# One kernel, two transformer layers of each of two kinds: experts' products kept together on TensorE, weights asked for earlier, low queries padded to full depth

## The chip, the cores and the metric

The kernel runs on one core of a Trainium2 chip. A core has five engines, each with its own queue of instructions: TensorE (PE, with its weight loader PEld), VectorE (DVE), ScalarE (ACT), GpSimd (POOL) and SyncE (SP, which issues most of the DMA transfers). The metric is the time on the device in microseconds (us), the median of the runs.

## The reference

The input is 512 tokens of 1024 numbers. Two layers of a first kind come first, then two of a second kind, all in float32.

A layer of the first kind projects the normed tokens, runs three mixers beside each other (an mLSTM in chunks, a causal attention with compressed keys, a gating over chunks), projects their outputs back and adds them to the tokens. After that comes a mixture of 32 experts, of which each token goes to two:

```python
def expert_block(args):
    rows, rw, e = args
    xi = x_pad[rows]
    h = jax.nn.silu(xi @ w1[e]) * (xi @ w3[e])
    return (h @ w2[e]) * rw[:, None]
```

Here w1 and w3 are 1024 x 256 and w2 is 256 x 1024 for each expert.

A layer of the second kind has an attention (dilated with 16 heads in the first, differential with 8 double heads in the second), a cross attention to 256 memory tokens and a feed-forward block. The scores of both attentions are a product of queries and keys over 64 numbers per head:

```python
sc = jnp.einsum('bhcqd,bhckd->bhcqk', qblk, k, preferred_element_type=f32) * scale
p = jax.nn.softmax(sc, axis=-1)
```

## The kernel before, in words

**Order of the work.** The class `Kern` writes every instruction to a `Recorder` (lines 86 to 381) in place of issuing it. `add` (157) notes what each operation reads and writes and derives from it what it depends on; `price` (209) gives its cost by engine and shape. At the end `flush` (245) plays the program through these costs and decides the order of each engine. For every engine it takes the ready operations, keeps those that can start by the earliest time at which any of them can, and picks the one of lowest rank (316). The rank is the place in the program, in steps of AGE (100, and 1000 within `moe`), less the operation's height, which is the cost of the longest chain behind it (286 to 291). Buffers are part of that plan: an operation that needs a new tile waits for a free slot of the pool (268 to 284). The order found is then issued, with the order on each engine fixed (366 to 378). The prices hold no cost for a change of a product's shape. All instructions of the program therefore bear the line of this issuing loop, L367, in the profile, and they are told apart by their tiles.

**Buffers.** The heap is 46 tiles of 128 x 1024 float32 (`H`, 470); `T2` gives half tiles, and all eight banks of PSUM are one pool (515, 518). Most products are made of three, with high and low halves of both operands in a rounded format (`mm3`, 534); weights come as `raw` and are split into `wh` and `wl` (`wload`, 561).

**Experts.** `run` (2260) does for each of the first two layers: the mixers and output projection (`f1`), the routing (`route`), the keys and values of a memory (`mem_kv`, whose results are stored to DRAM as `memk` and `memv`), the twelve loads of the first pair's weights (`pair_raw`, 2126, called at 2272), the overflow loop (`overflow`, 2044) and the experts (`moe`, 2145). The overflow loop is a wall: it is recorded as an operation of all engines (2102), reads its count on all of them, and starts when all are free; operations behind it in the program can be planned ahead of it only if its buffers stay free (280). Experts are worked on in 16 pairs per layer, 64 slots for each expert of the pair. For a pair, `prep_pair` (2175) gathers the 128 rows of tokens with an indirect DMA on POOL into `xg` and transposes them in eight blocks into `xe`; `up` (2187) does 32 products with w1 and w3, `down` (2202) transposes the result and does eight products with w2, and after every second pair `combine` (2226) adds the results to the tokens by eight sums of four products each. The two experts of a pair lie on the two halves of the output's partitions, so each product of `up` and `down` has 64 columns of weights:

```python
mm(ps[e * 64:(e + 1) * 64, g * 256:(g + 1) * 256], x[:, j * 128 + e * 64:j * 128 + (e + 1) * 64],
   w[:, j % 4 * 256:(j % 4 + 1) * 256], start=j == 0, stop=j == 7)
```

In the profile these are `mm<-raw,xe` (up, two instructions for each product) and `mm<-raw,t` (down, two as well); the combine products are `mm<-yh,pT` and `mm<-yl,pT`. The planner is free to set any other ready product between two of these.

**Attention.** `qkv_steps` (1084) projects queries, keys and values for half of the heads at a time (hb). For a block of 128 tokens it turns the queries by the rotary angles on POOL (1103), transposes them on TensorE and writes a high part `qh` on ScalarE (1115) and a low part `ql` on VectorE (1118). Of the even heads the high part of the query lies on partitions 0 to 63 and again on 64 to 127, against keys whose high part lies on one half of the partitions and whose low part on the other. The low query lies on its own 64 partitions alone, two blocks of tokens in one tile. `qk` (1133) is the product of both for a head: one product over 128 rows with `qh` (`mm<-kt,qh`) and one over 64 rows with `ql` (`mm<-kt,ql`):

```python
s.nc.tensor.matmul(out, q[:, e * 512 + h // 2 * 128:e * 512 + (h // 2 + 1) * 128], k[:, o], start=True, stop=False)
s.nc.tensor.matmul(out, l[a, h // 2 * 128:(h // 2 + 1) * 128], k[a, o], start=False, stop=True)
```

`longnet` (1141) and `diff` (1229) call it 64 times each, 128 in all, between the projections of the second half of the heads and the output projection of the first.

Of the kernel before, what the change touches and what calls it, by code (L numbers as in the profile page):

```python
# [10 lines left out]
F32 = mybir.dt.float32  # L11
# [54 lines left out]


class Op:
    __slots__ = ("i", "eng", "fn", "a", "k", "cost", "lat", "deps", "users", "left", "ready", "end", "new", "uses", "start", "rows", "load", "move", "age", "height", "rank")


class Engine:
# [13 lines left out]
class Recorder:  # L86
# [15 lines left out]
    def __init__(s, nc, tc):  # L102
        s.nc, s.tc = nc, tc
        s.ops, s.hist, s.first, s.keys = [], {}, {}, {}
        s.tensor, s.vector, s.scalar = Engine(s, "PE", nc.tensor), Engine(s, "DVE", nc.vector), Engine(s, "ACT", nc.scalar)
        s.gpsimd, s.sync = Engine(s, "POOL", nc.gpsimd), Engine(s, "SP", nc.sync)
        s.cache = {}


    def region(s, ap):  # L110
# [46 lines left out]
    def add(s, eng, method, fn, a, k, outs=None, ins=None):  # L157
        o = Op()
        if outs is None:
            outs = [v for n in ("out", "accum_out") for v in s.aps(k.get(n))]  # L160
            rest = list(a)
            if "out" not in k:
                outs += s.aps(rest.pop(0))
            ins = [v for x in rest for v in s.aps(x)] + [v for n, x in k.items() if n not in ("out", "accum_out") for v in s.aps(x)]
        o.i, o.eng, o.fn, o.a, o.k = len(s.ops), eng, fn, a, k
        o.age = s.AGE
        o.cost, o.lat = s.price(eng, method, outs, ins, k)
        o.move = None
        if isinstance(o.cost, tuple):

            o.move, (o.cost, o.lat) = (o.cost[1], o.lat), (o.cost[0], o.cost[1] + o.lat + 900)
        o.deps, o.users, o.new, o.uses = set(), [], [], []
        if eng == "PE":
            m = 1
            for v in ins[0].shape[1:]:
                m *= int(v)
            o.rows, o.load = int(ins[0].shape[0]) / 128, m * 0.417 * (1 if ins[0].dtype == BF16 else 4 if ins[0].dtype == F32 and method == "matmul" else 2)
        for ap, wr in [(x, False) for x in ins] + [(x, True) for x in outs]:
            t = ap.tensor
            if t.space == bass.MemoryType.DRAM and not hasattr(t, "cap_key"):  # L180
                continue
            name = t.name
            p0, p1, m = s.region(ap)
            h = s.hist.setdefault(name, ([], []))
            if t.space != bass.MemoryType.DRAM:
                if name not in s.first:
                    s.first[name] = o
                    tag = ((t.space, t.cap_key), name.split("_")[0] if t.space == PSUM else "")
                    s.keys.setdefault(tag, (int(t.bufs or t.tag_meta.bufs), []))[1].append(name)
                    o.new.append((name, tag))  # L190
                if name not in o.uses:
                    o.uses.append(name)
            for q, q0, q1, qm in h[0]:
                if q1 > p0 and p1 > q0 and qm & m:
                    o.deps.add(q)
            if wr or t.space == PSUM:

                for q, q0, q1, qm in h[1]:
                    if q1 > p0 and p1 > q0 and qm & m and (wr or s.ops[q].eng != eng):
                        o.deps.add(q)  # L200
            if wr:
                for x in h:
                    x[:] = [r for r in x if r[1] < p0 or r[2] > p1 or r[3] & ~m]
            h[wr is False].append((o.i, p0, p1, m))
        o.deps.discard(o.i)
        s.ops.append(o)
# [38 lines left out]
    def flush(s):  # L245
        ops = s.ops
        left = {}
        for o in ops:
            for n in o.uses:
                left[n] = left.get(n, 0) + 1  # L250
            o.left, o.ready, o.end = len(o.deps), 0.0, None
            for d in o.deps:
                ops[d].users.append(o)
# [40 lines left out]
        def next_wall():  # L294
# [6 lines left out]
                    n[tag_of[x][0]] = n.get(tag_of[x][0], 0) + 1  # L301
            return o.i, n
        wall, asked = next_wall()
        while len(order) < len(ops):
            best = None
            for e, hp in heaps.items():
                cand = []
                for i, o in hp[:s.WINDOW]:
                    t = start(o)
                    if t is not None:  # L310
                        cand.append((t, o))
                if not cand:
                    continue
                now = max(free.values()) if e == "ALL" else free[e]
                lim = max(now, min(c[0] for c in cand))
                t, o = min((c for c in cand if c[0] <= lim), key=lambda c: c[1].rank)
                pick = (t, o.i, o)
                if best is None or pick[:2] < best[:2]:
                    best = pick
            t, i, o = best  # L320
            heaps[o.eng].remove((i, o))
            o.new = [(n, tag_of[n]) for n in o.uses if n not in live]
            for n, tag in o.new:
                live.add(n)
# [132 lines left out]
class Kern:  # L457
# [626 lines left out]
    def qkv_steps(s, act, W, hb, kinds, Q, K, values, ready):  # L1084
# [4 lines left out]
        for kind in kinds:  # L1089
            toks = []  # L1090

            def consume(t, ps):
# [10 lines left out]
                s.apply_rope(nc.gpsimd, tok.rearrange("p (h c) -> p h c", h=8)[:, :, 0:16], s.rope2, t, 8, 8)  # L1103
                if kind == 0:
                    q = s.H(F32R, "qh")
                    l = s.H(F32R, "ql") if t % 2 == 0 else Q[hb, t - 1][2]
                    lv = l[:, (t % 2) * 512:(t % 2 + 1) * 512]
                    Q[hb, t] = q, lv, l
                    tp = s.TP()
                    for c in range(4):  # L1110
                        nc.tensor.transpose(tp[:, c * 128:(c + 1) * 128], tok[:, c * 128:(c + 1) * 128], s.ident)
                    for d in range(2):
                        for e in range(2):
                            a, b = slice(64 * e, 64 * e + 64), slice(64 * (e ^ d), 64 * (e ^ d) + 64)
                            nc.scalar.copy(q[b, e * 512:(e + 1) * 512], tp[a])
                    for e in range(2):
                        a, o = slice(64 * e, 64 * e + 64), slice(e * 512, e * 512 + 512)
                        nc.vector.tensor_sub(lv[a], tp[a], q[a, o])
                    return
                for c in range(4) if t == NT - 1 else ():  # L1120
                    tp = s.TP()
# [10 lines left out]

    def qk(s, out, Q, K, hb, t, h):

        q, l, _ = Q[hb, t]
        k, e = K[hb * 4 + h // 2], h % 2
        a, o = slice(64 * e, 64 * e + 64), slice(e * 512, e * 512 + 512)
        s.nc.tensor.matmul(out, q[:, e * 512 + h // 2 * 128:e * 512 + (h // 2 + 1) * 128], k[:, o], start=True, stop=False)
        s.nc.tensor.matmul(out, l[a, h // 2 * 128:(h // 2 + 1) * 128], k[a, o], start=False, stop=True)

    def longnet(s, act, nxt, xsrc):
        nc = s.nc
# [1002 lines left out]
    def moe(s, l, raws, nxt):  # L2145
# [40 lines left out]

        def up(p, w13):
            ps, x = s.PS("pa"), xe.pop(p)
            for g in range(2):
                for j in range(8):  # L2190
                    for e in range(2):
                        w = w13[g * 4 + j // 4 * 2 + e]
                        mm(ps[e * 64:(e + 1) * 64, g * 256:(g + 1) * 256], x[:, j * 128 + e * 64:j * 128 + (e + 1) * 64],
                           w[:, j % 4 * 256:(j % 4 + 1) * 256], start=j == 0, stop=j == 7)
            u = us[p] = s.T2()
            A.activation(u[:, 0:256], ps[:, 0:256], AF.Tanh, scale=0.5)
            V.scalar_tensor_tensor(u[:, 0:256], u[:, 0:256], 1.0, ps[:, 0:256], op0=ALU.add, op1=ALU.mult)
# [4 lines left out]
        def down(p):  # L2202
# [4 lines left out]
            A.copy(u[:, 256:512], tp[:, 0:256])  # L2207
            yb = s.PS("py"), s.PS("py")
            w = w2.pop(p)
            for hf in range(2):  # L2210
                for j in range(2):
                    for e in range(2):
                        mm(yb[hf][e * 64:(e + 1) * 64], u[:, 256 + j * 128 + e * 64:256 + j * 128 + (e + 1) * 64],
                           w[j * 2 + e][:, hf * 512:(hf + 1) * 512], start=j == 0, stop=j == 1)
            g, i = divmod(p, 4)
            _, tok, gate, _ = info[g]
            yh, yl = s.H(F32R, "yh"), s.H(F32R, "yl")
# [8 lines left out]
        def combine(last):  # L2226
            for t in range(NT):
                for hf in range(2):
                    pc = s.PS("pc")
                    n = len(ycur)  # L2230
                    for i, (pT, yh, yl) in enumerate(ycur):
                        for q, yy in enumerate((yh, yl)):
                            mm(pc, pT[:, t * 128:(t + 1) * 128], yy[:, hf * 512:(hf + 1) * 512], start=i == 0 and q == 0,
                               stop=i == n - 1 and q == 1)
                    xs = s.x[t][:, hf * 512:(hf + 1) * 512]
                    V.tensor_add(xs, xs, pc)
                if last:
                    nxt(t)
# [21 lines left out]
    def run(s):  # L2260
# [7 lines left out]
        for l in range(2):  # L2268
            s.f1(l, c.act, s.chain_route(l), I["x"][0] if l == 0 else s.xd)
            s.route()  # L2270
            kv.append(s.mem_kv(l))
            raws = [s.pair_raw(l, 0)]
            s.overflow(l)
            c = s.chain(I["attn_norm"][1] if l == 0 else I["mix_pre_g_2"][0], s.spill)
            s.moe(l, raws, c)
# [25 lines left out]
```

## Time and profile before

| | us |
|---|---|
| median of 3 runs | 2879.23 (2877.32 to 2879.76) |
| the profiled execution | 2878.05 |
| its span, first to last instruction | 2875.6 |
| first expert stage, about | 335 to 640 |
| second expert stage, about | 970 to 1275 |
| attention of the third layer, low queries in use | 1358 to 1560 |
| attention of the fourth layer, low queries in use | 2160 to 2335 |

The profile gives for each engine its busy time, for each group of instructions by tiles and shape (`out<-in partitions*columns`) their number and mean duration, the chain of work that ended last (followed back from the last instruction, at each step to what released it), and the instructions in order of time. A TensorE product's record runs from its start to a modelled end and overlaps the next one's, so durations are longer than the step from one start to the next; steps between starts are what TensorE's time is made of. The weight loader (PEld) works beside the products.

### The profile page before, as it was taken

The numbers are of one execution on the slowest core, as the hardware profiler recorded it, in microseconds if no ns is written. First come the engines' busy times: TensorE is split into PE (matmuls) and PEld (weight loads), VectorE is DVE, ScalarE is ACT, GpSimd is POOL, SyncE is SP. The second block draws the span as 40 slices with busy tenths as digits, with TensorE's granted clock in tenths as the row PEclk, the third lists the DMA queues.
The fourth block names the chain that finished last, engine by engine and source line by source line (L and its number), as shares of the span: only waits on it lengthen the run. The fifth ranks groups of instructions, "written<-read, shape, count | busy, mean of one in ns | idle before, by whom it ended". The sixth has DMA issues, their size and how long they took to land.

```text
span 2875.6 us, 40755 instructions
## 1 busy us (share of the span) xinstructions
PE 2796.2 (97%) x15208; PEld 2166.7 (75%) x15208; DVE 1519.1 (53%) x3279; ACT 1178.3 (41%) x2414; POOL 619.4 (22%) x720
## 2 busy tenths in 40 slices
PE   8999999999999999999999999999999999999998
PEld 7878655559888655557777888888877778888887
DVE  6686433337686243344588564343447685633433
ACT  5565111115555011135587462242356664622421
POOL 2523000003423000002344221001224442210012
PEclk9999999999999999999999999999999999999999
DMA  6035899953135799951013232232321232312321
GB/s 171 23 94 171 302 352 351 374 180 117 39 117 192 275 402 338 363 194 51 30 52 126 85 105 67 81 117 78 122 82 44 67 110 81 108 62 88 118 83 57
DMA packets 224057, 421.94 MB, mean 147 GB/s; under 512 B 46064, under 2 KB 112368, under 8 KB 223856
## 3 DMA queue, kind: packets, MB, share of 16 engines
q1 hardware_dynamic: 219248, 410.89, 41.3%
q0 software_dynamic: 4608, 8.40, 0.8%
q8 instruction: 122, 2.00, 0.3%
q14 instruction: 79, 0.65, 0.1%
HBM read 410.83 MB, written 16.78 MB: 149 GB/s over the span
## 4 chain that ended last, share of the span: by engine, by line
PE 80%; DVE 4%; ACT 2%; POOL 1%; DMA 1%; issue 1%; DVEq 0%; another core or an unknown queue 0%; POOLq 0%; ACTq 0%
PE mm L367 74%; PE tp L367 7%; DVE wl L367 1%; ACT t L367 1%; DVE x L367 1%; DMA raw<-w 1%; DVE t L367 1%; DMA xg<-xm,slidx 0%; POOL ra L367 0%; DVE y L367 0%; ACT qh L367 0%; ACT wh L367 0%; POOL pring L367 0%; DVE xnm L367 0%; DVE n_r L367 0%
## 5 line engine op out<-in xcount | busy, mean ns | idle before, releaser
L367 PE MATMUL mm<-wh,xth 128*128 128x512 f32 (+3 forms) x1088 | 406.6, 398 | 0.0
L367 PE MATMUL mm<-wl,xth 128*128 128x512 f32 (+3 forms) x1088 | 403.7, 396 | 0.8 <-DVE wl L367 0.8
L367 PE MATMUL mm<-wh,xtl 128*128 128x512 f32 (+3 forms) x1088 | 403.5, 395 | 0.0
L367 PE MATMUL mm<-xth,wh 128*128 128x512 f32 (+2 forms) x1216 | 377.7, 361 | 0.2
L367 PE MATMUL mm<-xtl,wh 128*128 128x512 f32 (+2 forms) x1216 | 376.4, 359 | 0.0
L367 PE MATMUL mm<-xth,wl 128*128 128x512 f32 (+2 forms) x1216 | 375.6, 359 | 0.0
L367 DVE SCALAR_TENSOR_TENSOR wl<-raw,pre_g,wh 128x512 fp32r<-128x512 f32 (+4 forms) x400 | 287.8, 760 | 149.5 <-ACT wh L367 119.5
L367 PE MATMUL mm<-raw,xe 128*64 128x256 f32 x2048 | 294.2, 387 | 0.0
L367 ACT ACTIVATE wh<-raw,pre_g 128x512 fp32r<-128x512 f32 (+4 forms) x400 | 251.8, 684 | 62.4 <-DMA raw<-w_gate_up 47.0
L367 PEld LDWEIGHTS mm<-xth,wh 128*128 128x128 f32 (+1 forms) x1216 | 222.6, 188 | 35.5 <-ACT xth L367 0.7
L367 PEld LDWEIGHTS mm<-xtl,wh 128*128 128x128 f32 (+1 forms) x1216 | 222.8, 187 | 35.0 <-issue 0.3
L367 PEld LDWEIGHTS mm<-xth,wl 128*128 128x128 f32 (+1 forms) x1216 | 222.6, 187 | 35.2 <-issue 0.3
L367 PEld LDWEIGHTS mm<-wh,xth 128*128 128x128 f32 x1088 | 204.4, 188 | 38.0 <-issue 5.9
L367 PEld LDWEIGHTS mm<-raw,xe 128*64 128x64 f32 x2048 | 157.1, 137 | 100.6 <-issue 30.0
L367 PEld LDWEIGHTS mm<-wl,xth 128*128 128x128 f32 x1088 | 204.2, 189 | 37.0 <-issue 4.6
L367 PEld LDWEIGHTS mm<-wh,xtl 128*128 128x128 f32 x1088 | 204.4, 188 | 35.9 <-issue 3.9
L367 POOL TENSOR_TENSOR ffl<-t,ffh 128x512 fp32r<-128x512 f32 x44 | 60.6, 1380 | 543.9 <-ACT ffh L367 505.9
L367 DVE TENSOR_TENSOR wl<-raw,wh 128x1024 fp32r<-128x1024 f32 x112 | 143.5, 1286 | 51.7 <-ACT wh L367 47.4
L367 PE MATMUL mm<-raw,t 128*64 128x512 f32 x512 | 137.3, 614 | 7.5 <-ACT t L367 7.4
L367 DVE TENSOR_TENSOR x<-x,mm 128x512 f32<-128x512 f32 x136 | 91.3, 684 | 84.6 <-PE mm L367 84.3
L367 ACT CAST wh<-raw 128x1024 fp32r<-128x1024 f32 (+2 forms) x128 | 120.1, 953 | 33.3 <-DMA raw<-w_down 31.2
L367 DVE SCALAR_TENSOR_TENSOR yl<-mm,slgate,yh 128x512 fp32r<-128x512 f32 x64 | 47.8, 749 | 161.1 <-ACT yh L367 151.1
(337 smaller groups left out, 4961.9 us busy)
## 6 DMA issues: line engine op xcount, KB each, us to landing
raw<-w SPq DMA_DIRECT2D x384, 512.0 KB
raw<-w_gate_up SPq DMA_DIRECT2D x176, 256.0 KB
raw<-w_down SPq DMA_DIRECT2D x40, 512.0 KB
raw<-x_wkv SPq DMA_DIRECT2D x32, 512.0 KB
raw<-a_w_in SPq DMA_DIRECT2D x24, 512.0 KB
raw<-b_w_in SPq DMA_DIRECT2D x24, 512.0 KB
raw<-w_in SPq DMA_DIRECT2D x24, 384.0 KB
raw<-w_out SPq DMA_DIRECT2D x16, 512.0 KB
```

The costliest lines, as they stand in the source:

```text
L367: r = o.fn(*o.a, **o.k)
```

## The change

Four things are changed. The recorder gets `together`: operations recorded within it form a group; the first of the group takes over the dependences on operations ahead of the group and all tiles of the others, and once it is placed, its engine takes the rest of the group next, in order. `up` makes two groups (w1, w3) of 16 products, `down` one of eight, `combine` one of four for each of its sums. `run` calls `pair_raw` for two pairs ahead of the overflow loop. The low queries get a tile of their own for each block, laid out like one copy of the high ones; the 64 partitions that hold nothing are filled with zeros on POOL, and `qk` takes both products over 128 rows.

```diff
+    def together(s, fn, *a):
+        s.run = object()
+        fn(*a)
+        s.run = None
...
     def flush(s):
+        head = None
+        for o in ops:
+            if o.group is None or head is None or head.group is not o.group:
+                head = last = o
+                continue
+            head.deps |= {d for d in o.deps if d < head.i}
+            head.uses += [n for n in o.uses if n not in head.uses]
+            o.deps.add(last.i)
+            last.next = last = o
...
-                for i, o in hp[:s.WINDOW]:
+                for i, o in hp[:s.WINDOW] if forced.get(e) is None else [(forced[e].i, forced[e])]:
...
+            forced[o.eng] = o.next
...
                 if kind == 0:
                     q = s.H(F32R, "qh")
-                    l = s.H(F32R, "ql") if t % 2 == 0 else Q[hb, t - 1][2]
-                    lv = l[:, (t % 2) * 512:(t % 2 + 1) * 512]
-                    Q[hb, t] = q, lv, l
+                    l = s.H(F32R, "ql")
+                    Q[hb, t] = q, l
+                    for e in range(2):
+                        nc.gpsimd.memset(l[64 - 64 * e:128 - 64 * e, e * 512:(e + 1) * 512].bitcast(F32), 0.0)
...
-                        nc.vector.tensor_sub(lv[a], tp[a], q[a, o])
+                        nc.vector.tensor_sub(l[a, o], tp[a], q[a, o])
...
-        s.nc.tensor.matmul(out, q[:, e * 512 + h // 2 * 128:e * 512 + (h // 2 + 1) * 128], k[:, o], start=True, stop=False)
-        s.nc.tensor.matmul(out, l[a, h // 2 * 128:(h // 2 + 1) * 128], k[a, o], start=False, stop=True)
+        for i, x in enumerate(Q[hb, t]):
+            s.nc.tensor.matmul(out, x[:, e * 512 + h // 2 * 128:e * 512 + (h // 2 + 1) * 128], k[:, e * 512:(e + 1) * 512], start=i == 0, stop=i == 1)
...
-            for g in range(2):
+            def part(g):
                 for j in range(8):
                     for e in range(2):
                         w = w13[g * 4 + j // 4 * 2 + e]
...
+            for g in range(2):
+                nc.together(part, g)
...
-            raws = [s.pair_raw(l, 0)]
+            raws = [s.pair_raw(l, p) for p in range(2)]
```

The loops of `down` and of `combine` (over the products of one sum) are wrapped in the same way.

## Rows read from the trace of the kernel before

**Rows 1.** The page, the chain that ended last, by engine.

```profile
PE 80%; DVE 4%; ACT 2%; POOL 1%; DMA 1%; issue 1%; DVEq 0%; another core or an unknown queue 0%; POOLq 0%; ACTq 0%
```

**Rows 2.** Groups by shape, TensorE: tiles, shape, count | busy us, mean ns | idle.

```profile
L367 PE MATMUL mm<-raw,xe 128*64 128x256 f32 x2048 | 294.2, 387 | 0.0
...
L367 PE MATMUL mm<-kt,ql 64*128 64x512 f32 x128 | 61.4, 499 | 0.0
```

**Rows 3.** Windows: length, busy PE, PEld, DVE, ACT, POOL, granted clock, DMA share, GB/s.

```profile
335.00:640.00 305.00, 292.51 (x1797) 168.94 (x1796) 98.38 (x197) 43.04 (x82) 13.78 (x14) 0.99 0.86 323
970.00:1275.00 305.00, 292.69 (x1782) 167.35 (x1781) 95.84 (x183) 42.35 (x80) 12.89 (x13) 0.99 0.86 327
1358.00:1560.00 202.00, 201.70 (x1020) 149.22 (x1018) 139.86 (x319) 143.35 (x300) 88.33 (x102) 1.00 0.16 53
2160.00:2335.00 175.00, 172.58 (x847) 125.69 (x846) 133.21 (x328) 112.91 (x239) 78.71 (x82) 0.98 0.17 55
```

**Rows 4.** Timeline, TensorE, first expert stage: start us, us from first start to last end.

```profile
379.24 0.65 PE L367 MATMUL mm<-raw,xe 128*64 128x256 f32 x2
379.82 0.38 PE L367 MATMUL tp<-const,xg 128*128 128x128 f32 x1
380.12 0.65 PE L367 MATMUL mm<-raw,xe 128*64 128x256 f32 x2
380.70 0.49 PE L367 MATMUL tp<-const,xg 128*128 128x128 f32 x2
```

**Rows 5.** Timeline, TensorE, later in the same stage.

```profile
456.23 0.39 PE L367 MATMUL mm<-yh,pT 128*128 128x512 f32 x1
456.55 1.95 PE L367 MATMUL mm<-raw,xe 128*64 128x256 f32 x16
458.43 0.73 PE L367 MATMUL mm<-yl,pT 128*128 128x512 f32 x2
459.00 0.39 PE L367 MATMUL mm<-yh,pT 128*128 128x512 f32 x1
459.23 0.40 PE L367 MATMUL mm<-yl,pT 128*128 128x512 f32 x1
```

**Rows 6.** Timeline, TensorE: first and last visit of 64 columns (of 173).

```profile
335.20 1.11 PE L367 MATMUL mm<-raw,xe 128*64 128x256 f32 x2
...
1271.64 3.70 PE L367 MATMUL mm<-raw,t 128*64 128x512 f32 x16 [0.46 <-ACT t L367]
```

**Rows 7.** Timeline, TensorE, attention of the fourth layer.

```profile
2272.10 0.40 PE L367 MATMUL mm<-wl,xth 128*128 128x512 f32 x1
2272.34 0.40 PE L367 MATMUL mm<-kt,qh 128*128 128x512 f32 x1
2272.66 0.50 PE L367 MATMUL mm<-kt,ql 64*128 64x512 f32 x1
2273.09 0.50 PE L367 MATMUL mm<-wh,xtl 128*128 128x512 f32 x1
2273.43 0.40 PE L367 MATMUL mm<-wh,xth 128*128 128x512 f32 x1
```

**Rows 8.** Timeline, weight loader, the same stretch; in brackets the idle time before.

```profile
2272.11 0.19 PEld L367 LDWEIGHTS mm<-kt,qh 128*128 128x128 f32 x1
2272.66 0.18 PEld L367 LDWEIGHTS mm<-kt,ql 64*128 64x128 f32 x1 [0.36 <-issue]
```

**Rows 9.** SP's first issues of experts' weights; two pieces of the chain (start, us).

```profile
290.74 0.87 SPq L367 DMA_DIRECT2D raw<-w  x2
...
324.11 7.10 DMA xg<-xm,slidx
...
465.89 6.41 DMA raw<-w
```

**Rows 10.** Windows, end of the fourth layer's attention, columns as in rows 3.

```profile
2300.00:2350.00 50.00, 49.50 (x277) 37.94 (x277) 47.29 (x116) 33.03 (x70) 26.45 (x19) 1.00 0.27 91
```

**Rows 11.** Groups by shape, GpSimd: tiles, shape, count | busy us, mean ns | idle.

```profile
L367 POOL TENSOR_TENSOR pring<-pring,l 128x512 f32<-128x512 f32 x80 | 87.0, 1091 | 184.2 <-DVE l L367 131.5 <-issue 23.9 <-PE mm L367 13.3
```

More of the change, by code (lines that the diff above doesn't have):

```diff
@@ L68 @@
 class Op:
-    __slots__ = ("i", "eng", "fn", "a", "k", "cost", "lat", "deps", "users", "left", "ready", "end", "new", "uses", "start", "rows", "load", "move", "age", "height", "rank")
+    __slots__ = ("i", "eng", "fn", "a", "k", "cost", "lat", "deps", "users", "left", "ready", "end", "new", "uses", "start", "rows", "load", "move", "age", "height", "rank", "group", "next")
 class Engine:
@@ L106, in __init__ @@
         s.gpsimd, s.sync = Engine(s, "POOL", nc.gpsimd), Engine(s, "SP", nc.sync)
-        s.cache = {}
+        s.cache, s.run = {}, None
+    def together(s, fn, *a):
+        s.run = object()
+        fn(*a)
+        s.run = None
     def region(s, ap):
@@ L165, in add @@
         o.i, o.eng, o.fn, o.a, o.k = len(s.ops), eng, fn, a, k
-        o.age = s.AGE
+        o.age, o.group, o.next = s.AGE, s.run, None
         o.cost, o.lat = s.price(eng, method, outs, ins, k)
@@ L303, in flush @@
         wall, asked = next_wall()
+        forced = {}
         while len(order) < len(ops):
@@ L1133, in qk @@
     def qk(s, out, Q, K, hb, t, h):
-        q, l, _ = Q[hb, t]
         k, e = K[hb * 4 + h // 2], h % 2
-        a, o = slice(64 * e, 64 * e + 64), slice(e * 512, e * 512 + 512)
-        s.nc.tensor.matmul(out, q[:, e * 512 + h // 2 * 128:e * 512 + (h // 2 + 1) * 128], k[:, o], start=True, stop=False)
-        s.nc.tensor.matmul(out, l[a, h // 2 * 128:(h // 2 + 1) * 128], k[a, o], start=False, stop=True)
+        for i, x in enumerate(Q[hb, t]):
+            s.nc.tensor.matmul(out, x[:, e * 512 + h // 2 * 128:e * 512 + (h // 2 + 1) * 128], k[:, e * 512:(e + 1) * 512], start=i == 0, stop=i == 1)
     def longnet(s, act, nxt, xsrc):
@@ L2209, in down, with part @@
             w = w2.pop(p)
[L2210 to L2214, printed above, removed]
+            def part():
+                for hf in range(2):
+                    for j in range(2):
+                        for e in range(2):
+                            mm(yb[hf][e * 64:(e + 1) * 64], u[:, 256 + j * 128 + e * 64:256 + j * 128 + (e + 1) * 64],
+                               w[j * 2 + e][:, hf * 512:(hf + 1) * 512], start=j == 0, stop=j == 1)
+            nc.together(part)
             g, i = divmod(p, 4)
@@ L2229, in combine, with part @@
                     pc = s.PS("pc")
[L2230 to L2234, printed above, removed]
+                    def part():
+                        n = len(ycur)
+                        for i, (pT, yh, yl) in enumerate(ycur):
+                            for q, yy in enumerate((yh, yl)):
+                                mm(pc, pT[:, t * 128:(t + 1) * 128], yy[:, hf * 512:(hf + 1) * 512], start=i == 0 and q == 0,
+                                   stop=i == n - 1 and q == 1)
+                    nc.together(part)
                     xs = s.x[t][:, hf * 512:(hf + 1) * 512]
```

## The prediction, as it was made before the result

> **What bounds the kernel now.** I read the page first. TensorE holds 80% of the chain that ended last, and no other engine more than 4% [rows 1]. So the order of TensorE's work is the time, and the question is what in that order is not arithmetic. The groups by shape name the three products that the change touches: the experts' up products (64 columns wide), the experts' down products (64 wide too) and the product with the low queries (64 rows deep) [rows 2, 6]. All others fill 96 or 128 rows and more than 64 columns of weights. I call a stretch of TensorE's order that holds only 64-column products, or only 64-row ones, a visit. The windows then show where they lie: two expert stages of 305 us each and two attention stages of 202 and 175 us, with TensorE busy in 96 to 100% of each [rows 3].
>
> The timeline gives the price of a visit. In the first expert stage one up product (two instructions) alternates with one transpose, and the period from one visit to the next is 380.12 - 379.24 = 0.88 us [rows 4]. In long visits an instruction costs 0.108 us, because two experts' products run side by side: from 456.55 to 458.43 sixteen of them take 1.88 us [rows 5], which is 16 x 0.108 = 1.73 and 0.15 for getting in. A turn with one transpose shows 0.38 and one with two 0.49, so a transpose costs 0.11 [rows 4]. So 0.88 holds 2 x 0.108 + 0.11 = 0.33 of work and **0.55 us of loss**. With an even number of products the loss is smaller: from 456.23 to 459.00 is 2.77 us, the work in it is one combine product (0.23), sixteen instructions (1.73) and two more combine products (0.46), together 2.42, so **0.35 us** is lost [rows 5]. The odd visit loses more, as its last product has no partner.
>
> I counted the visits of 64 columns in the timeline: 173 in both expert stages, the first at 335.20 and the last at 1271.64 [rows 6], 116 of them with an odd number of products. The loss is 116 x 0.55 + 57 x 0.35 = 63.8 + 20.0 = 84 us.
>
> The low queries are the same thing in the other direction. Around one of them TensorE's starts are 2272.34, 2272.66, 2273.09 and 2273.43: steps of 0.32, 0.43 and 0.34 [rows 7]. The step between two full products is 0.23 between two of the combine's (459.00 to 459.23 [rows 5]) and 0.24 just ahead. By the 0.23 that is 1.09 for what would be 0.69: **0.40 us lost per visit**. The weight loads show how: the load for the high queries begins at 2272.11, while the product begun at 2272.10 runs; that for the low ones begins only at 2272.66, after 0.36 us of idle loader [rows 7, 8]. There are 128 of these products; in five places two follow each other, so there are 123 visits and 123 x 0.40 = 49 us.
>
> **The change, part by part.**
>
> 1. *Runs stay together.* For each of 32 pairs of experts there are two groups of up products and one group of down products. No group can be cut, so there are at most 96 visits; a group that follows another group shares its visit, so at least 64 for an order that goes up, other work, down. Each group has an even number of products. I take 80 visits: 80 x 0.35 = 28 us in place of 84, a gain of 56 (ends: 96 visits, 50; 64 visits, 62). The instructions themselves stay, and the wait of the down products for ScalarE's copy (the last visit shows 0.46 us of it [rows 6]) stays too. The combine products are also kept together, four at a time; that moves nothing but the places of visits.
>
> What is late next are the weights. An expert stage moves 323 GB/s at a DMA share of 0.86 [rows 3], so 323/0.86 = 376 GB/s when full. The 192 loads of 0.524 MB of one layer are 100.7 MB, or 268 us at that rate. A stage of 305 - 28 = 277 us is only 9 us above this floor, although some loads land before it. The chain already has a load in it that cost 6.41 us [rows 9]. I give back 6 us a stage, one such wait, 12 in all (ends 0 and the whole 56). **Net 44.**
>
> 2. *Two pairs asked for ahead.* Twelve more loads go to SP's queue before the overflow loop, at 0.43 us an issue [rows 9], 5 us of SP's time. Behind them on SP are the stores of the memory's keys and values and the loop's own read; if a buffer isn't free, all of these wait for the TensorE product that frees it. On the path at that place is the gather of the first pair's tokens, 7.10 us [rows 9], not a weight. So the earlier loads can't start the stage sooner; they can slow the gather, whose packets then share the DMA engines with more loads, and they can save later waits of 6.41. I take **0** and keep as ends a gain of 13 (one such wait in each layer) and a loss of 7 (half a gather in each layer).
>
> 3. *Low queries padded.* With 128 rows the product has the shape of the high queries' product beside it, and I take its step of 0.23. It streams as many columns as before. The gross gain is 49 us, and three things take from it. First, VectorE: from 2300 to 2350 it is busy for 47.29 of 50 us [rows 10] while TensorE is busy for 49.50. Fourteen visits lie there, 14 x 0.40 = 5.6 us, and I count none of that as won. Elsewhere VectorE has 139.86 of 202 and 133.21 of 175 [rows 3], which leaves room for 25 and 20 us. Second, buffers: a low-query tile per token block instead of half of one is four tiles more of 46 in each stage, which can make a weight load late. Nothing of before shows it; the ends are 0 and one wait of 6.41 in each stage [rows 9], 13; I take 4, nearer the low end, since DMA is busy for only 0.16 there. Third, 32 fills with zeros on GpSimd, two behind each block's rotation. No row shows them; nothing and POOL's product of 512 elements bound one, 0 and 1.09 us [rows 11]. POOL is busy for less than half of both stages [rows 3], so they are hidden, except at a stage's start, where the first blocks wait for the rotation: ends 0 and 8 x 1.09 = 9, and I take 1. **Net 49 - 5.6 - 4 - 1 = 38.**
>
> The rows show a full product's weight load starting during the product ahead, on the same 128 rows [rows 7, 8]. The Trainium skill, TensorE: Matmul & The Clock Gate, Part 3 (Packing small matmuls, what overlaps and what doesn't), says that a weight load overlaps a product in flight only where the row groups differ. By that the padded product would still pay for its load in the open and part 3 would bring nothing: the sum would be 44 in place of 82. The trace disagrees, so this stays a rival.
>
> **Sum.** 44 + 0 + 38 = 82 us. The profiled execution took 2878.05 us, its span 2875.6, with 2.5 around it; that is 1.2 below the median of 2879.23, well inside what a measurement can tell (0.2%, some 6 us). 2878 - 82 = **2796 us**.
>
> **Rivals.**
> - *Weights pace the experts.* Loads wait for buffers as they do now, the stage stays at 323 GB/s, and TensorE stands where it used to switch. For it: DMA share 0.86 [rows 3]. Against: a share of 0.86 leaves room, and so does the floor of 268. Only part 3 is won: 2878 - 38 = 2840.
> - *Attention gains nothing*, because VectorE, ScalarE and the buffers hold it. For it: VectorE at 47.29 of 50. Against: TensorE was busy for 49.50 of 50 even there [rows 10]. 2878 - 44 = 2834.
> - *Each padded product pays its load in the open*, though the rows of the high queries say otherwise; part 3 brings nothing and the time is 2834 as well. (This is what the rule above would make of it.)
> - *Slower: TensorE stands inside the groups.* A run of up products needs four loads; now nothing can be put between its products while the last two are on their way. At full rate a load takes 0.524/376 = 1.39 us; two of them in each of the 64 up groups are 178 us. 2878 - 82 + 178 = 2974. It decides from a mean of 82/64 = 1.28 us per group on, about one load. Against: now TensorE is busy for 292.51 of 305 us there [rows 3].
> - *Nothing happens*: the planner fills the freed time with waits of its own, in the same lengths; 2878.
>
> **Chances.** Likeliest 0.71; weights 0.10; attention held 0.10; loads in the open 0.02; standing inside the groups 0.04; nothing 0.03. The likeliest alone spans from all gross gains and the best of part 2 (62 + 49 + 13 = 124, 2754) to both lower terms (50 - 24 + 25 = 51, 2827); its middle is 2765 to 2825. With the three cases at 2834 to 2840 added, **2765 to 2842** leaves out the last two and a little on each side. Faster by over 0.2%: 0.71 + 0.10 + 0.10 + 0.02 = 0.93; within 0.2%: 0.03; slower: 0.04.
>
> **What would show it.** The low queries' group should read 128 rows with a step of 0.23, and the idle loader before it should vanish; attention windows should be near 182 and 161 us. The timeline should show 64 to 96 visits of 64 columns, none with a single product. The expert stages should take about 283 us, at about 350 GB/s. Windows that don't shrink while TensorE's idle before the experts' products grows would show the first rival; VectorE near 95% in attention the second; gaps within runs of up products the slower one. The forecast is wrong if a visit's loss is hidden by something else that is late, so that stalls rise by what the visits lose.

## The result, and the profile of the changed kernel

The changed kernel takes 2786.58 us (median of 4 runs, 2782.92 to 2788.47) where the kernel before, run beside it, took 2878.52 (2877.32 to 2879.76): a ratio of 0.968, 95% interval 0.966 to 0.970. That is 92 us less. The forecast was 2796 us with a range of 2765 to 2842, and faster.

First the page of the changed kernel: span and instructions, busy shares by engine, and the chain that ended last by engine, which answers to [rows 1].

```profile
span 2781.0 us, 40797 instructions
...
PE 2689.4 (97%) x15208; PEld 2153.5 (77%) x15208; DVE 1518.6 (55%) x3279; ACT 1176.0 (42%) x2414; POOL 631.5 (23%) x752
...
PE 85%; DVE 6%; DMA 3%; ACT 3%; issue 2%; POOL 1%; SPq 0%; DVEq 0%; POOLq 0%; ACTq 0%
```

TensorE still bounds the kernel: it is 97% busy, and it holds a larger part of the chain than before. What became shorter lies inside its own busy time. The groups by shape say where (answering to [rows 2]; below them the fills that the change adds on GpSimd):

```profile
L385 PE MATMUL mm<-raw,xe 128*64 128x256 f32 x2048 | 235.0, 385 | 0.0
L385 PE MATMUL mm<-kt,ql 128*128 128x512 f32 x128 | 51.3, 407 | 0.0
...
L385 POOL MEMSET ql<- 64x512 f32 x32 | 16.6, 520 | 75.9 <-DMA raw<-w 68.2 <-PE mm L385 4.7 <-PE tp L385 1.8
```

The 2048 up instructions have the same mean duration as before (385 ns against 387), but the time in which at least one of them runs fell from 294.2 to 235.0 us. So no instruction became faster; there is less time around them. The low queries' products now read 128 rows and 407 ns, like a full product, in place of 499.

The windows answer to [rows 3]: length, busy time of PE, PEld, DVE, ACT, POOL, granted clock, DMA share, GB/s. The first two are the expert stages, the other two the attention stages that have low queries.

```profile
350.00:625.00 275.00, 264.27 (x1783) 160.32 (x1782) 107.80 (x214) 52.01 (x102) 13.44 (x14) 0.98 0.92 345
960.00:1233.00 273.00, 263.50 (x1798) 160.29 (x1795) 108.97 (x206) 52.52 (x102) 17.57 (x22) 0.98 0.91 351
1305.00:1487.00 182.00, 178.04 (x1011) 148.86 (x1010) 135.76 (x317) 139.68 (x295) 89.69 (x103) 1.00 0.18 58
2080.00:2238.00 158.00, 154.79 (x865) 130.45 (x864) 133.20 (x333) 113.64 (x244) 79.90 (x90) 1.00 0.18 59
```

The windows of before, 305, 305, 202 and 175 us, became 275, 273, 182 and 158. They are cut roughly. From the first low query's product to the last, the attention stages went from 200.8 to 182.6 and from 180.7 to 158.2 us; from the first up product to the last combine product, the expert stages went from 312.4 to 274.9 and from 319.4 to 273.7. The expert stages now move 345 to 351 GB/s in place of 323 to 327. TensorE's idle time in the attention windows grew a little, from 0.3 to 4.0 us and from 2.4 to 3.2; that is a part of the gain that the padding did not keep.

Where in TensorE's time did the span lose its 94.6 us? The page of before gives TensorE's busy time, in which at least one product runs:

```profile
PE 2796.2 (97%) x15208; PEld 2166.7 (75%) x15208; DVE 1519.1 (53%) x3279; ACT 1178.3 (41%) x2414; POOL 619.4 (22%) x720
```

It fell from 2796.2 to 2689.4, by 106.8 us, with the same 15208 products. The rest of the span, in which TensorE stands idle, grew from 79.4 to 91.6. **So the changes between kinds of product gave back 107 us, and 12 us of that went into new stalls**; the experiments show where these lie. In TensorE's order there are 66 visits of 64 columns in place of 173, none with an odd number of products (116 before), and no visit of 64 rows in place of 123. By the prediction's prices these visits cost 84 + 49 us before and 66 x 0.35 = 23 now, so 110 less, near the 106.8.

The timeline of TensorE in the first expert stage shows what a visit looks like now (start, us from the first start to the last end, instructions in it):

```profile
425.63 0.39 PE L385 MATMUL mm<-yl,pT 128*128 128x512 f32 x1
425.95 7.13 PE L385 MATMUL mm<-raw,xe 128*64 128x256 f32 x64
433.01 0.86 PE L385 MATMUL tp<-rt_rec,P 128*128 128x6 bf16 x28
```

Sixty-four up instructions, two groups behind one another, run in 7.13 us without a break: 0.111 us each, close to the 0.108 of long visits in [rows 5]. Before, a visit of two of them cost 0.88 us with one transpose [rows 4].

And the attention, TensorE and then its weight loader, answering to [rows 7, 8]:

```profile
1304.88 0.39 PE L385 MATMUL mm<-wh,xtl 128*128 128x512 f32 x1
1305.11 0.39 PE L385 MATMUL mm<-kt,ql 128*128 128x512 f32 x1
1305.34 0.39 PE L385 MATMUL mm<-wl,xth 128*128 128x512 f32 x1
```

```profile
1304.89 0.19 PEld L385 LDWEIGHTS mm<-kt,ql 128*128 128x128 f32 x1
1305.11 0.19 PEld L385 LDWEIGHTS mm<-wl,xth 128*128 128x128 f32 x1
```

The steps into and out of the low queries' product are 0.23 us. Its weights start loading at 1304.89, while the product that began at 1304.88 runs, and the loader is not idle ahead of it.

### The profile page after: what moved, and what is told of

The parts are those of the page before. It is cut to its first block, busy times and chain, and to the rows that moved or that the text cites. A ratio compares the mean times of both kernels' runs of the same rounds, so it can differ in the third digit from the quotient of the medians.

```text
span 2781.0 us, 40797 instructions
## 1 busy us (share of the span) xinstructions
PE 2689.4 (97%) x15208; PEld 2153.5 (77%) x15208; DVE 1518.6 (55%) x3279; ACT 1176.0 (42%) x2414; POOL 631.5 (23%) x752
## 4 chain that ended last, share of the span: by engine, by line
PE 85%; DVE 6%; DMA 3%; ACT 3%; issue 2%; POOL 1%; SPq 0%; DVEq 0%; POOLq 0%; ACTq 0%
PE mm L385 78%; PE tp L385 7%; DVE wl L385 2%; DMA xg<-xm,slidx 2%; DVE x L385 1%; ACT t L385 1%; DVE t L385 1%; DMA raw<-w 1%; ACT wh L385 0%; DVE nm L385 0%; ACT qh L385 0%; DVE pt L385 0%; DVE xtl L385 0%; ACT pring L385 0%; POOL t L385 0%
## 5 line engine op out<-in xcount | busy, mean ns | idle before, releaser
L385 DVE SCALAR_TENSOR_TENSOR wl<-raw,pre_g,wh 128x512 fp32r<-128x512 f32 (+4 forms) x400 | 286.0, 755 | 148.7 <-ACT wh L385 116.0
L385 PE MATMUL mm<-raw,xe 128*64 128x256 f32 x2048 | 235.0, 385 | 0.0
L385 PEld LDWEIGHTS mm<-raw,xe 128*64 128x64 f32 x2048 | 145.1, 138 | 84.2 <-issue 12.4
L385 ACT ACTIVATE t<-mm 128x256 f32<-128x256 f32 (+3 forms) x72 | 28.5, 403 | 244.9 <-PE mm L385 208.7
L385 PE MATMUL mm<-raw,t 128*64 128x512 f32 x512 | 123.3, 626 | 7.4 <-ACT t L385 7.4
L385 PE MATMUL mm<-wh,ffh 128*128 128x512 f32 x352 | 130.1, 389 | 0.0
```

Of the source, the lines that this page charges most:

```text
L385: r = o.fn(*o.a, **o.k)
```

## The experiments

The theory at this point: each visit costs what the prediction priced, the parts add up, and the early loads (part 2) do nothing. Four kernels take the change apart. They ran beside the same runs of the kernel before, whose median there was 2876.53 us. Under each expectation, "part" means the parts of the prediction.

**Padding alone**: the kernel before with only this edit.

```diff
-                    l = s.H(F32R, "ql") if t % 2 == 0 else Q[hb, t - 1][2]
+                    l = s.H(F32R, "ql")
+                    for e in range(2):
+                        nc.gpsimd.memset(l[64 - 64 * e:128 - 64 * e, ...], 0.0)
...
```

The rest of the edit is the change's own, in the low part's write and in `qk`.

> The kernel before with the padded low queries alone. Theory of the visits (each low product on 64 rows costs 0.4 us more than a full one, and nothing takes it back): 123 x 0.40 = 49 us less, 2825 to 2835, and attention windows of 202 and 175 us fall by about 22 us each. Rival, attention held by VectorE or by the four more buffers: less than 20 us gained, 2860 or more, with TensorE idle in those windows.

Measured: 2840.51 us, ratio 0.988 (0.985 to 0.990), 36.0 us less than before, short of the 49 that I expected. Its two attention windows, columns as above:

```profile
1362.00:1544.00 182.00, 178.95 (x1012) 149.77 (x1010) 136.19 (x316) 139.95 (x296) 89.89 (x103) 0.99 0.19 58
2138.00:2296.00 158.00, 154.81 (x866) 130.49 (x865) 133.42 (x333) 113.94 (x245) 80.08 (x90) 1.00 0.19 59
```

They have the lengths of the changed kernel's, 182 and 158 (from the first low query's product to the last 182.7 and 158.2), so the attention's part of the gain is the padding's and needs nothing of the rest.

**Runs together alone**: the kernel before with the groups in TensorE's order, one pair of weights ahead and unpadded queries. The edit of `up`, with those of `down`, `combine` and the recorder left out:

```diff
-            for g in range(2):
+            def part(g):
...
+            for g in range(2):
+                nc.together(part, g)
```

> The kernel before with the runs of the experts' products (and of the combine's) kept together, and neither the early loads nor the padding. Theory of the visits: 173 visits become 64 to 96, all even, 47 to 56 us less, 2822 to 2832. Rival, weights pace the experts: TensorE stands in the groups, less than 20 us gained, 2860 or more.

Measured: 2809.98 us, ratio 0.977 (0.974 to 0.979), 66.5 us less, more than the 47 to 56 that I expected. Its expert windows:

```profile
339.00:621.00 282.00, 271.24 (x1842) 167.71 (x1839) 109.70 (x222) 52.72 (x105) 14.31 (x16) 0.99 0.94 361
940.00:1226.00 286.00, 275.06 (x1842) 168.16 (x1842) 110.89 (x212) 52.74 (x103) 13.71 (x15) 0.98 0.92 358
```

From the first up product to the last combine product its two stages take 282.0 and 286.0 us; before they took 312.4 and 319.4. That is 30.4 + 33.4 = 64 of the 66.5 us. TensorE's order has 68 visits, all even, and its busy time on the page is 61.5 us less than before (2734.7), where 84 - 68 x 0.35 = 60 was to be saved by the price of a visit. The queues deliver 358 to 361 GB/s when TensorE asks for them, so the weights did not hold the experts.

**Early loads alone**: the kernel before with one line changed.

```diff
-            raws = [s.pair_raw(l, 0)]
+            raws = [s.pair_raw(l, p) for p in range(2)]
```

> The kernel before with two pairs of weights asked for ahead of the overflow loop, nothing else. Theory of the visits: TensorE's order keeps its visits, so within 13 us of before, 2865 to 2885. Rival, the early loads bring a good part of the gain (the experts were short of weights): 20 us or more less, 2858 or below.

Measured: 2896.81 us, ratio 1.0075 (1.0048 to 1.0102): 20.3 us **slower**, outside what I had allowed for this part.

**All but the early loads**: the changed kernel with that line put back.

```diff
-            raws = [s.pair_raw(l, p) for p in range(2)]
+            raws = [s.pair_raw(l, 0)]
```

> The changed kernel with one pair asked for ahead, as before. If the early loads only delay a gather (one wait of some 6 us in each expert stage of the changed kernel, on the second gather of tokens), this is up to 12 us faster than the changed kernel: 2774 to 2786. If they save later waits for weights, it is slower: 2790 to 2800.

Measured: 2773.00 us, ratio 0.965 (0.962 to 0.967): 13.6 us below the 2786.58 of the changed kernel, which was measured beside other runs of before. Its profiled execution is 10.0 us shorter than that of the changed kernel, so I take the loss as 10 to 14 us. The four runs of the one (2772.0 to 2777.5) and the eight of the other (2782.6 to 2788.5, with the repeat at the end) do not touch. Padding and runs add up almost exactly, 36.0 + 66.5 = 102.5 against 2876.53 - 2773.00 = 103.5, and the early loads take 10 to 14 of it back.

Where do they take it? The chain of the changed kernel has the gathers of the experts' tokens in it (start, us); in each layer the first pair's, then the second pair's:

```profile
333.40 5.08 DMA xg<-xm,slidx
...
340.08 9.06 DMA xg<-xm,slidx
...
944.37 4.07 DMA xg<-xm,slidx
...
950.11 8.20 DMA xg<-xm,slidx
```

The timeline of the same kernel, first SP's issues, then TensorE (idle time in brackets, with what ended it), shows what lies around them:

```profile
339.15 5.92 SPq L385 DMA_DIRECT2D raw<-w  x10
```

```profile
339.55 0.22 PE L385 MATMUL tp<-rt_rec,P 128*128 128x6 bf16 x2 [5.55 <-issue]
...
349.18 1.33 PE L385 MATMUL tp<-const,xg 128*128 128x128 f32 x5 [6.10 <-DMA xg<-xm,slidx]
350.44 1.12 PE L385 MATMUL mm<-raw,xe 128*64 128x256 f32 x4
...
958.35 1.33 PE L385 MATMUL tp<-const,xg 128*128 128x128 f32 x5 [6.64 <-DMA xg<-xm,slidx]
```

The wait that ends at 339.55 is the one at the overflow loop. The second pair's gather is issued at 340.08, behind the loop and among ten loads that SP puts out from 339.15 on. It takes 9.06 us. TensorE's order is fixed, the transposes of the second pair stand in it **ahead** of the first pair's up products, and so the whole stage waits for that gather: 6.10 us in one layer, 6.64 in the other, 12.7 together. In the kernel without the early loads the gathers are issued on GpSimd ahead of the loop (first two lines), and TensorE's first up products start at 336.36, 14 us earlier:

```profile
322.25 1.23 POOL L385 DMA_INDIRECT xg<-xm,slidx  x1 [13.22 <-DVEq L2075]
323.79 0.99 POOL L385 DMA_INDIRECT xg<-xm,slidx  x1 [0.30 <-remote]
```

```profile
333.55 1.97 PE L385 MATMUL tp<-const,xg 128*128 128x128 f32 x8 [7.49 <-issue]
336.36 1.12 PE L385 MATMUL mm<-raw,xe 128*64 128x256 f32 x4
...
935.26 2.40 PE L385 MATMUL tp<-const,xg 128*128 128x128 f32 x10 [4.59 <-issue]
```

Not all of the 14 us are lost: the loop itself stands 6 us later in the changed kernel (339.55 against 333.55), and TensorE worked until then. The idle time is the loss. Without the early loads there is one wait at the loop in each layer, 7.49 and 4.59 us, together 12.1. With them there are two behind each other, 5.55 + 6.10 and 4.59 + 6.64, together 22.9. The difference of 10.8 is nearly the whole difference of TensorE's idle time on the two pages, 91.6 against 80.2.

The wait at the loop is itself bound up with the gathers ahead of it: in the first layer TensorE starts again 1.1 to 1.2 us behind the landing of the last one, at 339.55 behind 333.40 + 5.08 = 338.48 in the changed kernel, and at 332.39 behind 324.11 + 7.10 = 331.21 [rows 9] before. By these times two gathers ahead of the loop share one wait, and a gather behind it gets one of its own. Why the planner puts the second gather behind the loop when the loads come early isn't shown.

The stages themselves are longer there (281.9 and 286.0 us against 274.9 and 273.7). At the end of the first it is 336.4 + 281.9 = 618.3 against 350.4 + 274.9 = 625.3, so 7.0 us earlier, and after the second stage 9.8 us (the last combine product starts at 1223.18 against 1232.94). The spans of the two profiled executions differ by 10.0. The loss is made in these two places.

The kernel with the early loads alone has the same wait, here TensorE's first transpose of its second pair:

```profile
348.82 0.48 PE L367 MATMUL tp<-const,xg 128*128 128x128 f32 x1 [6.10 <-DMA xg<-xm,slidx]
```

In the second layer it is 5.3 us. The two make 11.4 of its 20.3; besides, its order has 185 visits in place of 173, which at 0.35 to 0.55 is 4 to 7 us more. The pages agree with both: idle time rose by 10.9 us (90.3 against 79.4) and busy time by 6.7 (2802.9 against 2796.2).

**Low products of 64 rows on padded tiles.** This keeps the fills, the buffers and everything else of the change, and lets only the low queries' products read their 64 filled rows. It takes the price of the narrow products apart from what the padding costs.

```diff
-        for i, x in enumerate(Q[hb, t]):
+        a = slice(64 * e, 64 * e + 64)
+        for i, x in enumerate(Q[hb, t]):
+            p = a if i else slice(0, 128)
-            s.nc.tensor.matmul(out, x[:, ...], k[:, ...], ...)
+            s.nc.tensor.matmul(out, x[p, ...], k[p, ...], ...)
```

> The changed kernel with the low product taken over its own 64 partitions again, out of the same padded tiles: zeros, buffers and, but for a few places, the order stay. Theory of the visits (the shape alone costs 0.40 us a visit): 118 to 128 visits, 47 to 51 us more than the changed kernel's 2786, so 2830 to 2838. Rival, the gain of the padding came from another plan around it: under 2805.

Measured: 2826.78 us, ratio 0.982 (0.980 to 0.984), some 40 us slower than the changed kernel at 2786, where I expected 47 to 51. (This kernel and the next three ran beside a median of before of 2877.03, the last two beside 2875.90.) The timeline has the old steps again:

```profile
1311.60 0.39 PE L385 MATMUL mm<-kt,qh 128*128 128x512 f32 x1
1311.91 0.50 PE L385 MATMUL mm<-kt,ql 64*128 64x512 f32 x1
1312.34 0.50 PE L385 MATMUL mm<-wh,xth 128*128 128x512 f32 x1
1312.68 0.39 PE L385 MATMUL mm<-kt,qh 128*128 128x512 f32 x1
```

From 1311.60 to 1312.68 is 1.08 us for three steps, 0.39 more than 3 x 0.23. The fills and the four more buffers are still there, so all 40 us are the shape of 123 lone products, 0.33 each on the path. TensorE's busy time is 50.1 us longer than in the changed kernel (2739.5 against 2689.4), or 0.41 a visit, and its idle time 6.3 us shorter.

**Up products in pairs.** The changed kernel with sixteen groups of two experts' products each in place of two long ones, so that other work may come between them:

```diff
-                for j in range(8):
-                    for e in range(2):
+                for e in range(2):
...
             for g in range(2):
-                nc.together(part, g)
+                for j in range(8):
+                    nc.together(part, g, j)
```

> The changed kernel with the up products held together in groups of two (one of each expert) in place of sixteen. Its order on TensorE has 106 visits in place of 66, none odd. If an even visit costs 0.35 us: 40 x 0.35 = 14 more, 2796 to 2804. Rival, only odd visits cost (the missing partner): 2783 to 2790. Rival, every visit costs the 0.55 of an odd one: 2808 or more.

Measured: 2796.20 us, ratio 0.972 (0.970 to 0.974), 10 us slower than the changed kernel where I expected 14. The order has 106 visits, all even, in place of 66; TensorE's busy time is 16.9 us more (2706.3 against 2689.4), 16.9/40 = 0.42 a visit, and its idle time 4.5 us less. The timeline of TensorE has a short visit of this sort by itself:

```profile
364.64 0.65 PE L385 MATMUL mm<-raw,xe 128*64 128x256 f32 x4
365.22 0.49 PE L385 MATMUL tp<-const,xg 128*128 128x128 f32 x2
365.64 0.65 PE L385 MATMUL mm<-raw,xe 128*64 128x256 f32 x4
```

The period is 1.00 us, and 4 x 0.108 + 2 x 0.11 = 0.65 of it is work: 0.35 of loss, the price that [rows 5] gave. So it is the number of visits, not the groups as such, that costs.

**Gathers recorded ahead of the loop**, without and with the early loads. If the loss of the early loads is the second gather behind the loop, it goes when both gathers stand ahead of it. In the step that runs the layers the call of the loop is taken out, and the experts' step makes it itself:

```diff
+        for p in range(2):
+            prep_pair(p)
+        s.overflow(l)
-        prep_pair(0)
...
-                prep_pair(p + 1)
+                if p:
+                    prep_pair(p + 1)
```

> The changed kernel with one pair of loads ahead, as in the run without early loads, and the gathers of the first two pairs of experts recorded ahead of the overflow loop. If TensorE's idle time around the loop (7.5 and 4.6 us there) is partly the gather's: 2760 to 2770; if it is all the loop's own: 2771 to 2777.

> The same, with two pairs of loads ahead of the loop, as in the changed kernel. If the early loads cost only through the second gather, which stands behind the loop and behind a burst of loads in the changed kernel, they cost nothing here: within 4 us of the kernel with the gathers ahead and one pair of loads, or faster. Rival, they cost through buffers and a later loop: 8 to 15 us slower than that kernel.

Measured: with one pair asked for ahead 2786.62 us, ratio 0.968 (0.967 to 0.970); with two pairs 2771.07, ratio 0.963 (0.961 to 0.964). GpSimd's timeline of the second shows both gathers ahead of the loop, and TensorE's that the experts start before it and are broken off once by it:

```profile
323.97 1.46 POOL L385 DMA_INDIRECT xg<-xm,slidx  x1 [7.90 <-DVE P L385]
325.74 1.17 POOL L385 DMA_INDIRECT xg<-xm,slidx  x1 [0.30 <-issue]
```

```profile
336.03 2.37 PE L385 MATMUL mm<-raw,xe 128*64 128x256 f32 x18
344.32 1.98 PE L385 MATMUL mm<-raw,xe 128*64 128x256 f32 x8 [5.92 <-issue]
```

With the gathers ahead, the kernel with early loads is 2786.62 - 2771.07 = 15.5 us **faster** than the one without, as fast as the kernel without early loads that has the loop first; with the second gather behind the loop they cost 10 to 14. So it is not the loads themselves that cost, it is what the order puts behind them. That early loads win 15.5 is not shown by this: the kernel that they are compared with is itself slower than expected (2760 to 2777). The version with two pairs is the fastest of all, but its interval (0.961 to 0.964) and that of the kernel without early loads (0.962 to 0.967) overlap, and I don't tell the two apart. Both beat the changed kernel.

One thing is left open: why the gathers ahead with one pair are 13.6 us slower than the same kernel with the loop first. In the profiled executions it is 3.3 us behind at the end of the first expert stage (the last combine product starts at 621.18 against 617.92), 5.2 at the end of the second and 9.3 at the end of the span, so the loss has no one place. TensorE's idle time is 8.9 us longer (89.1 against 80.2): the wait at the loop is 6.71 us against 7.49 in the first layer but 7.48 against 4.59 in the second, where the store of the memory's values ends it; gathers cost waits of 1.17 and 1.76 us, and there is one of 2.84 for GpSimd behind the second stage. The planner writes a new order for each kernel, and why this one has these waits isn't shown.

**Turn first**: the two gathers ahead, two pairs of weights, and the transposes and ScalarE's copy of a pair recorded ahead of the next pair's up products, so that the copy is done when the down products come.

```diff
-        def down(p):
+        def turn(p):
...
+            if p > 0:
+                turn(p - 1)
             up(p, w13)
```

> The kernel with gathers ahead and two pairs of loads ahead, and the transposes and ScalarE's copy for a pair's down products recorded ahead of the next pair's up products, where before they stood directly ahead of the down products. In the changed kernel 26 visits begin with a down product that shows 0.4 to 0.5 us of idle time for ScalarE's copy. If that wait is on the path: 26 to 30 x 0.45 = 12 to 13 us less, 2755 to 2762, with at most 70 visits. Rival, the planner only trades it for more visits (70 in place of 68) or another wait: 2768 to 2776.

Measured: 2773.59 us, ratio 0.965 (0.963 to 0.966); no gain over 2771.07. TensorE's idle time that the copy ends went from 9.0 us in 17 places to 8.0 in 18. In 22 of the 32 pairs TensorE's order still has no up product between the transposes and the down products (30 of 32 before this edit): the planner orders by its own costs. So the wait of the down products is not won by the place in which they are recorded.

**The changed kernel once more**, beside the last three.

> The changed kernel itself, beside the others on the same chip: 2782 to 2789.

Measured: 2785.90 us, ratio 0.968 (0.966 to 0.970), 0.7 below the first set's median.

## Why the prediction was right, point by point

- **Visits price the runs.** Right in kind, and short by 22 us: net 44 was forecast, 66.5 was measured. I won 56 gross by 80 visits; the order has 66 to 68, so 84 - 68 x 0.35 = 60, and the runs alone brought 64 us in the stages and 66.5 in all. The term that was wrong is the give-back of 12 us to the weights. It rested on a full rate of 376 GB/s worked out from a share, and a floor of 268 us. The page of before has a slice of 72 us, within the second expert stage, at 402 GB/s, so 376 was not the most that the queues give, and the runs show stages of 274 to 286 us at 345 to 361 GB/s and no such wait. The price was misread too: 6.41 us is how long the load stands in the chain [rows 9], from 465.89 to 472.30. TensorE's idle time there was 1.13 us:

```profile
472.30 0.51 PE L367 MATMUL tp<-const,t 128*128 128x128 f32 x2 [1.13 <-DMA raw<-w]
```

- **Early loads cost nothing.** This is the step that failed. I had a gather right, as the thing on the path at that place [rows 9], and half a gather a layer as the upper end, 7 us in both. The loss was 10 to 14, outside the ends. But I took the gather of 7.10 us for the first pair's. GpSimd's timeline of before shows two, and the one on the path, at 324.11, is the second:

```profile
322.57 1.23 POOL L367 DMA_INDIRECT xg<-xm,slidx  x1 [13.22 <-DVEq L2058]
324.11 0.99 POOL L367 DMA_INDIRECT xg<-xm,slidx  x1 [0.31 <-remote]
```

  So what I had not asked is where the *second* pair's gather goes: before, it was issued ahead of the loop, and with the loads it came behind, with its transposes in front of the first run of products and a wait of 6.10 and 6.64 us of its own.
- **Padding wins 38.** Measured: 36.0 alone and 2809.98 - 2773.00 = 37.0 with the runs. The gross price of 0.40 a visit (49 us) holds: putting only the shape back makes TensorE busy for 50.1 us more. On the path that is 40 us, as 6.3 us of idle time go with it, which the padding had brought; 3.7 and 0.8 us of it lie in the two attention windows. Waits there name GpSimd's rotation and the two engines that make the softmax's tiles. The attention windows, forecast near 182 and 161 us, are 182 and 158.
- **The load in the open** did not come: the load at 1304.89 runs beside the product begun at 1304.88, on the same 128 rows, and the steps are 0.23 us. By the rule of the Trainium skill (TensorE: Matmul & The Clock Gate, Part 3) that load would have waited; here it is contradicted for loads of 128 rows.
- **The mechanism behind both wins.** The runs show that a change between shapes of product costs time: 0.35 us for a visit with an even number of 64-column products, 0.40 for a lone product of 64 rows. The Trainium skill, TensorEngine Tiling (Array Packing), Key Properties, says that changing the tiling mode drains the TensorE. The trace agrees in that the changes between shapes have a price, of 0.35 to 0.55 us; that the time goes into draining is not something it shows.
- **The rivals.** Weights pacing the experts: against it the windows' 275 and 273 us at higher rates. Attention held: its windows shrank. Standing inside the groups: a visit of 64 instructions runs in 7.13 us without a gap. That the end fits to 10 us is in part luck, two errors against each other: 22 us too little for the runs and 10 to 14 too little lost on the early loads.
- **The range.** Its upper end rests on a sum, 50 - 24 + 25 = 51, whose 24 and 25 no line before works out, and which leaves out the loss of 7 us that part 2 gave as an end. The measured time lies far from that end.

## What to carry to other kernels

Look in TensorE's order for products that don't fill the array among ones that do: each visit costs 0.35 to 0.55 us here, and TensorE counts as busy in that time (97% before and after). Keep such products in long runs, or pad them to the full shape where a fill costs less than the change. When a load is moved earlier, look at what its queue and the program's order now put behind it; the same loads cost 10 to 14 us in one order and nothing in another. And read a wait's price from the engine's idle time: a load that stood in the chain for 6.41 us had stopped TensorE for 1.13.

## What the runs showed that I had not expected

- A visit with an odd number of 64-column products loses 0.55 us against 0.35. Its last product has no partner in the other half of the columns: the two instructions of a lone product start 0.27 us apart (379.240 and 379.507 in the kernel before), those of two experts' products 0.006 (381.117 and 381.123).
- The gathers issued among a burst of loads took 9.06 and 8.20 us, those just before the burst 5.08 and 4.07. The median of all 32 in the changed kernel is 7.3, so it is the early two that are short, and the place of the gather cost more than its length.
- Two products of 64 rows that follow each other on different halves of the rows ran side by side in the kernel before: two of them start at 2165.703 and 2165.706, and the next instruction at 2166.135, so both took 0.43 us together. It happened in five places only.
- Asking for two pairs of loads ahead changed the time by 10 to 14 us one way and by 15.5 the other, while the bytes stayed the same. The first is traced to a gather; the second is not explained.
